# A hybrid SSD and attention block on one core: out_proj's third block of rows is loaded before the attention ends, gate's first operands after it, and a pair of weight casts is queued sooner

## The chip, the cores and the metric

The kernel runs on one core of one Trainium2 chip. The metric is the device time of one execution in microseconds (us); lower is better. The profiler adds its own record of one execution: what each engine did and when. The engines are named as in the profile: PE (TensorE, matrix multiplies), PEld (its weight loads), DVE (VectorE), ACT (ScalarE), POOL (GpSimd) and SP (SyncE, which here only issues DMAs).

## What is computed

One layer of a streaming encoder on a sequence of 1024 tokens of width 1024, all in float32:

```python
h = rms_norm(x, pre_mix_gain)
z, xbc, dt, q, k, v = split(h @ w_in)
y_ssd = ssd_group(z, xbc, dt)          # convolution, chunked state-space scan, gate by silu(z), norm
y_sb  = stick_breaking(q, k, v)        # 8 heads of 64, then a norm over each head
mix = concat([y_ssd, y_sb]) @ w_out    # "out_proj"
x = x + rms_norm(mix, post_mix_gain)
h = rms_norm(x, pre_ffn_gain)
f = (silu(h @ w_gate) * (h @ w_up)) @ w_down
x = x + rms_norm(f, post_ffn_gain)
```

## The kernel before, in words

Every large product keeps float32 accuracy by splitting each operand into a high part (a cast, on ACT, line 74) and a low part (the difference, on DVE, line 75) and adding three matmuls (`mm3`, lines 78 to 80: high by high, high by low, low by high). A matmul here is 128 x 128 by 128 x 512. The kernel is one program without loops at run time; Python writes it out, and a scheduler decides the order of the instructions of each engine by readiness and priority. What an engine does is then strictly in that order. `tc.issue_after(ins)` puts what is written inside it behind `ins` on the engine of `ins`; it is an order, not a wait. `tc.high_priority` moves what is inside it ahead.

The work has these stages, with their times in the profiled execution:

1. *Merged stage*, to about 505 us: in_proj, the SSD group and the attention are interleaved by `merge`, and at its end the first two blocks of out_proj (`stage("wo")` and `stage("o01")`). out_proj works on blocks of 128 tokens, p = 0 to 7, from the end of the sequence. A block needs its eight 128 x 128 pieces of y, normed and split, in a pair of tiles `yhl` (high and low).
2. *out_proj and its norms*, to about 592 us: the loop over p at line 1158. `run(p)` issues block p's 48 matmuls into two PSUM banks `po`; `out_tail(p - 2)` transposes on PE the result of two blocks earlier; `out_norm(p)` loads the block's rows of x, 512 KB, into `x1` (line 1091, SP), squares `po` on ACT (line 1095), makes the norm's factor (lines 913 to 918), multiplies by the gain `gm_b` on DVE (line 1101), adds x (line 1102), squares again (line 1104), stores x1 by POOL (line 1105) and multiplies by `g2_b` (line 1110, tile `tm`, the operand of the transposes). The two gain rows are loaded once, broadcast over 128 partitions to 512 KB each, by DMAs that ACT issues (line 923), and scaled on ACT (line 924).
3. *gate and up*: a Strassen-like scheme of seven products for each pair of feature blocks, a "quad" (`quad`, `step`). Each `step` of a quad takes two operands, gate's and up's, from the list `lops`. The first quad's first operands are `eo` (four loads of 256 KB by `early_load`, cast by `early_ops`); the second's and third's are the `heads` (loaded by `head_load`, cast by `left_gen` when `pump` asks for them).
4. *down*, to the end.

`out_load(p, part)` (lines 801 to 835) brings a block's y in: two loads of y into the low tile of `yhl` (lines 823 and 828, 256 KB each), four loads of norm factors into `Rb` (lines 825 and 832, each row broadcast over 64 or 128 partitions), three multiplies of the two on DVE (lines 826 and 834), the cast on ACT and the difference on DVE. `Rb` has one buffer for all blocks from 1 on (the tile of tag "Rb", line 822), so a block's factors can only be loaded when the difference of the block before it is done.

Where a block's `yhl` lies matters for the change. Block 1, 6 and 7 share two buffers of the pool `wo` (line 813), on the side of the memory where in_proj's weights were, free when in_proj's last matmul is done. Blocks 2 to 5 lie in the tiles of four later operands (line 811: T3h, T3l, T2h, T2l), in a pool that is opened where the attention's tiles were, so they can be written only after the attention's last use of those. The two gain rows, `x1`, `tm` and `eo` lie there too.

`rows_rstd(0, i)` (lines 788 to 799) makes the norm factors `r_d` of the tokens of blocks 4 to 7 from sums that the attention stores last; those of blocks 1 to 3 exist earlier.

Of the kernel before, what the change touches and what calls it, by code (L numbers as in the profile page):

```python
# [48 lines left out]
def tile_hybrid_block(  # L49
# [731 lines left out]
    def load_wo(i):  # L781
        for k, c in enumerate(KO):
            hi, lo = woh[k][i], wol[k][i]
            A.activation(hi, f32(lo), AF.Copy, scale=g_mix[:, c : c + 1])
            V.scalar_tensor_tensor(lo, f32(lo), g_mix[:, c : c + 1], f32(hi), ALU.mult, ALU.subtract)  # L785
            yield 0, 0.6
# [14 lines left out]
    def out_load(p, part):  # L801


        sb = NB - 1 - p
        n, csl = sb // 4, slice(P * (sb % 4), P * (sb % 4) + P)
        if p not in blk:
            if p == 0:
                blk[p] = tuple(big.tile([P, 8, P], F32R, tag=x, name="yhl") for x in ("G", "dec"))
            else:
                if 2 <= p < 6:  # L810
                    yhl = rpA.tile([P, 2, 8, P], F32R, tag=("T3h", "T3l", "T2h", "T2l")[p - 2], name="yhl")
                else:
                    yhl = wo.tile([P, 2, 8, P], F32R, tag="yhl", name="yhl", bufs=2)
                blk[p] = yhl[:, 0], yhl[:, 1]
        yh, yl = blk[p][:2]
        y_v = y_d[n].rearrange("c p s -> p c s")
        g0, g1, k0 = {"early": (0, 1, 0), "late": (1, 2, 6), "all": (0, 2, 0)}[part]
        k1 = 4 + 2 * g1
        if part == "late":
            Rb = pre.tile([P, 2, P], F32, name="Rb2")  # L820
        else:
            Rb = (pre.tile([P, 6, P], F32, name="Rb0") if p == 0 else wo.tile([P, 8, P], F32, tag="Rb", name="Rb"))[:, 0:k1]
            nc.sync.dma_start(f32(yl[:, 0:4]), y_v[:, 4:8, csl])
            for h in range(2):
                nc.sync.dma_start(Rb[64 * h : 64 * h + 64, 0:4], r_d[n][0][4 * h : 4 * h + 4, csl].partition_broadcast(64))
            V.tensor_tensor(Rb[:, 0:4], f32(yl[:, 0:4]), Rb[:, 0:4], ALU.mult)
        kg = 4 + 2 * g0
        nc.sync.dma_start(f32(yl[:, kg:k1]), y_v[:, 2 * g0 : 2 * g1, csl])
        R4 = Rb[:, kg - k0 :].rearrange("p (g k) s -> p g k s", k=2)
        y4 = f32(yl[:, kg:k1]).rearrange("p (g k) s -> p g k s", k=2)  # L830
        for g in range(g0, g1):
            nc.sync.dma_start(R4[:, g - g0, 1], r_d[n][g][8 - 8 * g, csl].partition_broadcast(P))
        for k in range(2):
            V.tensor_tensor(R4[:, :, k], y4[:, :, k], R4[:, :, 1], ALU.mult)
        split(yh[:, k0:k1], yl[:, k0:k1], Rb)
# [12 lines left out]
    def stage(t):  # L848
        nonlocal wo
        if t[0] in "xz" and t < "z2":  # L850

            with tc.issue_after(stored[0].ins):
                next(copied, None)
                if t[0] == "z" or t > "x3":
                    next(copied, None)
        if t[:3] == "qkv":
            yield from proj_qkv(int(t[3]), st[int(t[3])])
        elif t[0] == "x":
            yield from conv_tile(int(t[1]))
        elif t == "ssd":  # L860
            side.append(ssd())
            yield 0, 0.1
        elif t == "z23":
            yield from z_last()
        elif t[0] == "z":
            if t == "z0":
                yield from flush()
            yield from proj(t, z_evac(int(t[1])), 1.8)
        elif t == "r0":
            rows_rstd(1, 0, t2, tag="t2")  # L870
            yield 0, 1
        elif t == "wo":
            yield from flush()
            right_w.close()
            wo = es_w.enter_context(tc.tile_pool(reuse_waits="tile", name="wo", bufs=1, side="right"))
            fetch_wo(1)
            out_load(0, "late")
            out_load(1, "all")
            side.append(load_wo(1))
            yield 0, 3  # L880
        elif t == "o01":
            yield from out_mm(0, (0,), (0, 6))
            yield from out_mm(0, (0,), (6, 8))
            yield from out_mm(1, (0,))
            yield from flush()
            yield from out_mm(0, (1,))
            yield from out_mm(1, (1,))
# [182 lines left out]
    with es_o:  # L1070
# [15 lines left out]
        def out_norm(p):  # L1086
# [1 line left out]
            ssl = slice(P * sb, P * sb + P)  # L1088
            pm = blk.pop(p)[2]
            x1 = op.tile([P, D], F32, tag="x1", name="x1")  # L1090
            nc.sync.dma_start(x1, x[ssl, :])
            ssq = small_p.tile([P, 2], F32, tag="ssq", name="ssq")
            t = op.tile([P, D], F32, tag="tm", name="tm", bufs=2)
            for n in range(2):
# [59 lines left out]
        for i in range(2):  # L1154
            rows_rstd(0, i, op, tag="hT", bufs=1)
        ts = {}
        out_load(2, "all")
        for p in range(NB - 1):
            if p > 1:
                run(p)  # L1160
# [7 lines left out]
            if 2 < p + 2 < NB:  # L1168
                out_load(p + 2, "all")
            if p == 5:  # L1170
                raw = early_load()

        run(NB - 1)
        es_w.close()
# [13 lines left out]
        step(0)  # L1188
        p1_u = evac[0]
        with tc.issue_after(p1_u.ins):  # L1190
            next(tail, None)
        with tc.high_priority(offset=URGENT):
            next(norm)
# [2 lines left out]
        with tc.high_priority(offset=URGENT):  # L1196
            next(norm, None)
        a00 = step(0)
        with tc.issue_after(p1_u.ins):
            pump(2)  # L1200
        step(1)
        p1_u = evac[0]
        with tc.high_priority(offset=URGENT), tc.issue_after(last_mm[0].ins):
# [263 lines left out]
```

## Time and profile before

| | us |
|---|---|
| median of 3 runs | 1236.88 (1235.38 to 1238.39) |
| the profiled execution, its own time | 1237.42 |
| its span, first to last instruction | 1235.7 |
| PE busy | 1193.2 (97% of the span) |
| DVE busy | 929.3 (75%) |
| ACT busy | 588.2 (48%) |
| POOL busy | 92.8 (8%) |
| the 16 DMA engines, over the span | 157 GB/s |

A busy PE is not a PE at its peak: the same matmul is recorded at different lengths and distances, and what counts is how far the starts of neighbouring matmuls lie apart. The views that matter are the list of who waited for whom, cut to a stretch of time; the timeline of one engine; the groups of one tile; and the busy time by window. A row of the timeline has the start in us, the duration, the engine, the line, the operation, what it writes and reads, the count, and in brackets the time the engine stood idle before it and what released it. SPq and ACTq are the DMA issues of SP and ACT.

### The profile page before, as it was taken

To read this page: it belongs to the slowest core of one execution; us is meant where nothing else is said; L and a number is where in the kernel's file an instruction comes from. 1 tells how busy PE (TensorE), PEld (TensorE's weight loads), DVE (VectorE), ACT (ScalarE), POOL (GpSimd) and SP (SyncE) were. 2 spreads that over 40 slices of the span, in tenths; PEclk is the share of its full clock that TensorE was granted. 3 is DMA by queue.
4 is the path that set the end of the run, shared out by engine and by line. 5 is a ranking of instruction groups with operands and counts; after the bars stand their busy time and mean duration, and the time that the engine had idled before them with its cause. 6 is when DMAs were issued, how large, how long until landed. Compare 5 with 4: busy or idle time off the path is not lost.

```text
span 1235.7 us, 16325 instructions
## 1 busy us (share of the span) xinstructions
PE 1193.2 (97%) x5641; PEld 971.1 (79%) x5641; DVE 929.3 (75%) x1466; ACT 588.2 (48%) x1124; POOL 92.8 (8%) x232
## 2 busy tenths in 40 slices
PE   9998999999999999799999999999999999999997
PEld 7776778887887776578788888888888888888885
DVE  7478988778997978366898765565665558998877
ACT  7347555555654677345653333332333325444543
POOL 0041110000100100011200000000000000000000
PEclk9998999999999999899999999999999999999999
DMA  6794464455557345663973223223133298233346
GB/s 192 195 353 125 111 175 132 137 152 177 158 168 199 111 136 148 209 206 134 323 212 128 88 75 103 86 76 94 54 101 102 72 327 308 65 124 105 100 136 238
DMA packets 144731, 189.53 MB, mean 153 GB/s; under 512 B 10900, under 2 KB 97140, under 8 KB 144648
## 3 DMA queue, kind: packets, MB, share of 16 engines
q1 hardware_dynamic: 133392, 157.47, 41.5%
q0 software_dynamic: 7424, 25.17, 5.5%
q10 hardware_dynamic: 3832, 5.84, 1.3%
q8 instruction: 44, 0.72, 0.2%
q14 instruction: 39, 0.32, 0.1%
HBM read 138.52 MB, written 55.16 MB: 157 GB/s over the span
## 4 chain that ended last, share of the span: by engine, by line
PE 74%; DVE 11%; DMA 6%; ACT 4%; issue 3%; SPq 1%; POOL 0%; DVEq 0%; ACTq 0%; POOLq 0%
PE pd L79 5%; PE pd L78 5%; PE pd L80 5%; DVE sn L605 3%; PE o L628 2%; PE tp L616 2%; PE peu L80 2%; PE pcu L80 2%; PE pcg L80 2%; PE peg L80 2%; PE pcg L79 2%; PE peu L78 2%; PE pcu L78 2%; PE peg L79 2%; PE peg L78 2%
## 5 line engine op out<-in xcount | busy, mean ns | idle before, releaser
L74 ACT CAST flhi<-fraw 128x512 fp32r<-128x512 f32 x98 | 60.2, 621 | 153.7 <-PE pcg L79 35.6
L79 PE MATMUL pd<-folo,fohi 128*128 128x512 f32 x260 | 101.4, 390 | 0.2 <-DVE folo L75 0.2
L78 PE MATMUL pd<-fohi 128*128 128x512 f32 x260 | 101.4, 390 | 0.0
L80 PE MATMUL pd<-fohi,folo 128*128 128x512 f32 x260 | 101.2, 389 | 0.0
L605 DVE TENSOR_TENSOR_SCAN sn<-sn,smask 128x1024 f32<-128x1024 f32 (+3 forms) x64 | 87.4, 1366 | 17.8 <-ACT sn L601 17.5
L75 DVE TENSOR_TENSOR fllo<-fraw,flhi 128x512 fp32r<-128x512 f32 x98 | 66.9, 686 | 29.1 <-ACT flhi L74 29.1
L601 ACT ACTIVATE sn<-zp,msc 128x512 f32<-128x512 f32 (+2 forms) x96 | 56.0, 584 | 37.5 <-PE zp L600 33.7
L74 ACT CAST fohi<-rt 128x512 fp32r<-128x512 f32 x83 | 48.7, 618 | 47.7 <-PE pd L79 27.9
L78 PE MATMUL po<-woh,yhl 128*128 128x512 f32 x128 | 52.6, 411 | 10.4 <-ACT yhl L74 10.2
L620 ACT CAST wh<-tp 128x512 fp32r<-128x512 f32 (+1 forms) x80 | 42.6, 544 | 39.0 <-PE tp L616 38.5
L75 DVE TENSOR_TENSOR folo<-rt,fohi 128x512 fp32r<-128x512 f32 x83 | 55.2, 695 | 7.0 <-ACT fohi L74 7.0
L74 ACT CAST flhi<-fs 128x512 fp32r<-128x512 f32 x44 | 27.3, 622 | 69.7 <-PE peg L79 34.9
L621 DVE TENSOR_TENSOR wl<-tp,wh 128x512 fp32r<-128x512 f32 (+1 forms) x80 | 49.8, 628 | 10.5 <-ACT wh L620 10.2
L78 PEld LDWEIGHTS pd<-fohi 128*128 128x128 f32 x260 | 48.8, 188 | 10.6 <-ACT fohi L74 0.4
L79 PEld LDWEIGHTS pd<-folo,fohi 128*128 128x128 f32 x260 | 48.8, 188 | 10.5 <-DVE folo L75 0.5
L602 ACT ACTIVATE sp<-zp,msc 128x512 f32<-128x512 f32 (+2 forms) x96 | 55.8, 582 | 2.5 <-PE tp L616 2.4
L80 PEld LDWEIGHTS pd<-fohi,folo 128*128 128x128 f32 x260 | 48.8, 188 | 10.1
L79 PE MATMUL po<-wol,yhl 128*128 128x512 f32 x128 | 52.1, 407 | 1.2 <-DVE wol L785 1.2
L616 PE MATMUL tp<-ident,sp 128*128 128x128 f32 x288 | 47.9, 277 | 5.4 <-DVE sp L606 4.9
L78 PE MATMUL pj_x<-hh,wh_x 128*128 128x512 f32 x128 | 52.5, 410 | 0.0
L80 PE MATMUL po<-woh,yhl 128*128 128x512 f32 x128 | 51.5, 403 | 0.7 <-DVE yhl L75 0.7
L1065 POOL DMA_DIRECT2D a_d<-sg x44 | 23.8, 540 | 376.9 <-DVE sg L1064 376.8
(426 smaller groups left out, 3474.6 us busy)
## 6 DMA issues: line engine op xcount, KB each, us to landing
ps<-a_d SPq DMA_DIRECT2D x55, 256.0 KB
fraw<-in_w_gate_dram SPq DMA_DIRECT2D x22, 512.0 KB
fraw<-in_w_up_dram SPq DMA_DIRECT2D x22, 512.0 KB
a_d<-sg POOLq DMA_DIRECT2D x44, 256.0 KB, 2.6
rt<-in_w_down_dram SPq DMA_DIRECT2D x33, 256.0 KB
rt<-a_d SPq DMA_DIRECT2D x22, 256.0 KB
ps<-in_w_down_dram SPq DMA_DIRECT2D x22, 256.0 KB
xt<-in_x_t_dram SPq DMA_DIRECT2D x8, 512.0 KB
```

The lines of the kernel that those rows point to most:

```text
L74: A.copy(hi, src)
L75: V.tensor_tensor(lo, src, f32(hi), ALU.subtract)
L78: T.matmul(ps, lhsT=ah, rhs=bh, start=start, stop=False, skip_group_check=more)
L79: T.matmul(ps, lhsT=ah, rhs=bl, start=False, stop=False, skip_group_check=more)
L80: last_mm[0] = T.matmul(ps, lhsT=al, rhs=bh, start=False, stop=stop, skip_group_check=more)
L601: A.activation(sn[:, 1 + off : 1 + off + cw_], zp[:, 0:cw_], AF.Sigmoid, scale=rqn[:, qb : qb + 1])
L602: A.activation(sp[:, off : off + cw_], zp[:, 0:cw_], AF.Sigmoid, scale=rqp[:, qb : qb + 1])
L605: V.tensor_tensor_scan(sn[:, 1 : 1 + W], sn[:, 1 : 1 + W], smask[:, 0:W], 1.0, ALU.mult, ALU.max)
L616: T.transpose(tp[:, P * i : P * i + P], ws[a][:, co : co + P], ident)
L620: A.copy(wh[:, 0:n_], tp[:, 0:n_])
L621: V.tensor_tensor(wl[:, 0:n_], tp[:, 0:n_], f32(wh[:, 0:n_]), ALU.subtract)
L628: T.matmul(o[:, 0:cw_], lhsT=vv[:, k, h, :], rhs=wt[:, c0 : c0 + cw_], start=(first and k == kb + 1 and wt is wh), stop=(last and k == kb ...
```

## The change

Four edits, all around the border of stages 1, 2 and 3:

- Block 2's `yhl` comes from the pool `wo` instead of the tile T3h, so that blocks 1, 2, 6 and 7 share its two buffers; blocks 3, 4 and 5 move up by one tile each (T3h, T3l, T2h), and T2l is no longer used for this.
- `out_load(2, "all")` is called in the merged stage, right after block 1's, instead of after the attention.
- `early_load`, the four loads of `eo`, is put on SP behind the load of x of block 5 (`stored[0]` now remembers the last load of line 1091).
- The casts of the second quad's heads, made by `pump(2)` after the second `step(0)`, are made by `pump(3)` after the first, so that they stand one step earlier in the program.

One line is added in `stage`, so the lines from there to the end of `out_norm` and `out_tail` have numbers one higher in the changed kernel (1101 becomes 1102).

```diff
--- before.py
+++ after.py
@@ -807,8 +807,8 @@
             if p == 0:
                 blk[p] = tuple(big.tile([P, 8, P], F32R, tag=x, name="yhl") for x in ("G", "dec"))
             else:
-                if 2 <= p < 6:
-                    yhl = rpA.tile([P, 2, 8, P], F32R, tag=("T3h", "T3l", "T2h", "T2l")[p - 2], name="yhl")
+                if 3 <= p < 6:
+                    yhl = rpA.tile([P, 2, 8, P], F32R, tag=("T3h", "T3l", "T2h")[p - 3], name="yhl")
                 else:
                     yhl = wo.tile([P, 2, 8, P], F32R, tag="yhl", name="yhl", bufs=2)
                 blk[p] = yhl[:, 0], yhl[:, 1]
@@ -877,6 +877,7 @@
             out_load(0, "late")
             out_load(1, "all")
             side.append(load_wo(1))
+            out_load(2, "all")
             yield 0, 3
         elif t == "o01":
             yield from out_mm(0, (0,), (0, 6))
@@ -1088,7 +1089,7 @@
             ssl = slice(P * sb, P * sb + P)
             pm = blk.pop(p)[2]
             x1 = op.tile([P, D], F32, tag="x1", name="x1")
-            nc.sync.dma_start(x1, x[ssl, :])
+            stored[0] = nc.sync.dma_start(x1, x[ssl, :])
             ssq = small_p.tile([P, 2], F32, tag="ssq", name="ssq")
             t = op.tile([P, D], F32, tag="tm", name="tm", bufs=2)
             for n in range(2):
@@ -1154,7 +1155,6 @@
         for i in range(2):
             rows_rstd(0, i, op, tag="hT", bufs=1)
         ts = {}
-        out_load(2, "all")
         for p in range(NB - 1):
             if p > 1:
                 run(p)
@@ -1168,7 +1168,8 @@
             if 2 < p + 2 < NB:
                 out_load(p + 2, "all")
             if p == 5:
-                raw = early_load()
+                with tc.issue_after(stored[0].ins):
+                    raw = early_load()
 
         run(NB - 1)
         es_w.close()
@@ -1188,6 +1189,7 @@
         step(0)
         p1_u = evac[0]
         with tc.issue_after(p1_u.ins):
+            pump(3)
             next(tail, None)
         with tc.high_priority(offset=URGENT):
             next(norm)
@@ -1196,8 +1198,6 @@
         with tc.high_priority(offset=URGENT):
             next(norm, None)
         a00 = step(0)
-        with tc.issue_after(p1_u.ins):
-            pump(2)
         step(1)
         p1_u = evac[0]
         with tc.high_priority(offset=URGENT), tc.issue_after(last_mm[0].ins):
```

The scheduler turns this into other orders on the engines. Three places follow; in each, what stands there before and what stands there now. The numbers at the ends of names tell tiles of one name apart.

SP, from the attention's last store of y (line 635) on. `yhl_5245` is block 2's, `yhl_5330` with `Rb_5331` block 3's, `x1_5258` and `x1_5294` are the rows of x of blocks 0 and 1, `rt0` is the tile in which `rows_rstd` makes its factors. Before:

```order
L635 DMA y_d0_108<-osb3_4073 128x512
L823 DMA yhl_5684<-y_d0_108 128x4x128
L1078 DMA eo_5816<-eo_d0_146 128x512
L1078 DMA eo_5818<-eo_d1_147 128x512
L1078 DMA eo_5820<-eo_d2_148 128x512
L792 DMA rt0_5227<-ss_d09_130 36x128
L823 DMA yhl_5245<-y_d1_109 128x4x128
L828 DMA yhl_5245<-y_d1_109 128x4x128
L1091 DMA x1_5258<-in_x_dram 128x1024
L1091 DMA x1_5294<-in_x_dram 128x1024
L823 DMA yhl_5330<-y_d1_109 128x4x128
L799 DMA r_d09_134<-rt0_5227 36x128
```

Now:

```order
L635 DMA y_d0_108<-osb3_4073 128x512
L792 DMA rt0_5240<-ss_d09_130 36x128
L1092 DMA x1_5258<-in_x_dram 128x1024
L1092 DMA x1_5294<-in_x_dram 128x1024
L823 DMA yhl_5330<-y_d1_109 128x4x128
L825 DMA Rb_5331<-r_d19_136 64x4x128 x2
L799 DMA r_d09_134<-rt0_5240 36x128
L828 DMA yhl_5330<-y_d1_109 128x4x128
L832 DMA Rb_5331<-r_d19_136 128x128
L832 DMA Rb_5331<-r_d11_137 128x128
L792 DMA rt1_5249<-ss_d01_131 4x128
L823 DMA yhl_5448<-y_d0_108 128x4x128
```

The three eo loads and block 2's two loads of y have left this place, and block 3's loads of factors (`Rb_5331`), which stood behind the second `rt` load, now stand ahead of it.

DVE, the last rows ahead of block 3's difference (line 75, the last row). `x_5258` and `x_5294` are blocks 0 and 1, `tm<-po` is line 1101 or 1102 of block 1, `Rb<-yhl,Rb` are block 3's multiplies. Before:

```order
L915 SCALAR_TENSOR_TENSOR v<-ssq,e 128x1
L798 TENSOR_TENSOR rt_5236<-rt_5236 4x128
L916 SCALAR_TENSOR_TENSOR t<-y_5283,v 128x1
L916 SCALAR_TENSOR_TENSOR t<-y_5301,v 128x1
L918 SCALAR_TENSOR_TENSOR r<-t,y_5283 128x1
L834 TENSOR_TENSOR Rb<-yhl,Rb 128x2x128
L1110 SCALAR_TENSOR_TENSOR tm<-x_5258,r,g_b 128x512 x2
L918 SCALAR_TENSOR_TENSOR r<-t,y_5301 128x1
L834 TENSOR_TENSOR Rb<-yhl,Rb 128x2x128
L1101 SCALAR_TENSOR_TENSOR tm<-po,r,gm_b 128x512 x2
L1102 TENSOR_TENSOR x_5294<-x_5294,tm 128x512 x2
L75 TENSOR_TENSOR yhl<-Rb,yhl 128x1024
```

Now:

```order
L834 TENSOR_TENSOR Rb<-yhl,Rb 128x2x128
L798 TENSOR_TENSOR rt_5249<-rt_5249 4x128
L916 SCALAR_TENSOR_TENSOR v<-ssq_5274,e 128x1
L916 SCALAR_TENSOR_TENSOR v<-ssq,e 128x1
L917 SCALAR_TENSOR_TENSOR t<-y_5283,v 128x1
L917 SCALAR_TENSOR_TENSOR t<-y_5301,v 128x1
L919 SCALAR_TENSOR_TENSOR r<-t,y_5283 128x1
L919 SCALAR_TENSOR_TENSOR r<-t,y_5301 128x1
L1111 SCALAR_TENSOR_TENSOR tm<-x_5258,r,g_b 128x512 x2
L1102 SCALAR_TENSOR_TENSOR tm<-po,r,gm_b 128x512 x2
L1103 TENSOR_TENSOR x_5294<-x_5294,tm 128x512 x2
L75 TENSOR_TENSOR yhl<-Rb,yhl 128x1024
```

Block 3's second multiply (the first row; the first multiply stands two rows above it) stands now ahead of the factors of both blocks, and no longer behind block 0's line 1110, so that the cast on ACT that reads both can run earlier. The difference stands, as before, behind block 0's line 1110 (now 1111) and block 1's four operations.

ACT, around the casts of the second quad's heads (`flhi<-head`). `tm_6021` is block 7, `hT` are copies of transposes. Before:

```order
L1104 ACTIVATE tm_6021,ssq2_6100<-x1_6018 128x512 x2
L913 ACTIVATE e_6140<-ssq2_6100 128x1
L74 CAST T2h_5214<-pt_6025 128x4x128
L914 ACTIVATE y0_6138<-ssq2_6100,e_6140 128x1
L74 CAST T3h_5216<-pt_6031 128x4x128
L1125 COPY hT_6108<-pt_6110 128x512
L1125 COPY hT_6109<-pt_6116 128x512
L74 CAST flhi_6173<-head_6010 128x512
L74 CAST flhi_6177<-head_6012 128x512
L74 CAST flhi_6181<-head_6014 128x512
L74 CAST flhi_6185<-head_6016 128x512
L1063 ACT_TABLE_LOAD
```

Now:

```order
L1105 ACTIVATE tm_6021,ssq2_6116<-x1_6018 128x512 x2
L914 ACTIVATE e_6156<-ssq2_6116 128x1
L74 CAST flhi_6080<-head_6010 128x512
L915 ACTIVATE y0_6154<-ssq2_6116,e_6156 128x1
L74 CAST flhi_6084<-head_6012 128x512
L74 CAST flhi_6088<-head_6014 128x512
L74 CAST flhi_6092<-head_6016 128x512
L74 CAST T2h_5227<-pt_6025 128x4x128
L74 CAST T3h_5229<-pt_6031 128x4x128
L1126 COPY hT_6124<-pt_6126 128x512
L1126 COPY hT_6125<-pt_6132 128x512
L1064 ACT_TABLE_LOAD
```

The four head casts stand ahead of the two T2 and T3 casts and of the two copies `hT` that they stood behind.

## The prediction

> **What bounds the kernel now.** The first lines of the profile's page say that PE is nearly always occupied, so a gain can only come from the few places where it stands still or runs at a lower clock.
>
> ```profile
> span 1235.7 us, 16325 instructions
> PE 1193.2 (97%) x5641; PEld 971.1 (79%) x5641; DVE 929.3 (75%) x1466; ACT 588.2 (48%) x1124; POOL 92.8 (8%) x232
> ```
>
> Next the waits of PE alone, cut to the stretch that the change touches: the first two rows from 500 to 600 us (out_proj), the last two from 590 to 690 (gate). Columns: total, times, longest.
>
> ```profile
> PE po L78 <- ACT yhl L74: 10.2, 2, 8.1
> PE po L80 <- DVE yhl L75: 0.7, 2, 0.5
> PE pag L80 <- DVE fllo L75: 1.2, 1, 1.2
> PE pag L78 <- ACT flhi L74: 0.3, 1, 0.3
> ```
>
> So PE waits 10.9 us for blocks of out_proj (yhl) and 1.5 us for head casts. PE's timeline says where:
>
> ```profile
> 504.92 0.39 PE L80 MATMUL po<-woh,yhl 128*128 128x512 f32 x1
> 513.39 0.80 PE L78 MATMUL po<-woh,yhl 128*128 128x512 f32 x1 [8.09 <-ACT yhl L74]
> 519.10 0.47 PE L80 MATMUL po<-woh,yhl 128*128 128x512 f32 x1
> 529.42 0.50 PE L80 MATMUL po<-woh,yhl 128*128 128x512 f32 x1 [0.54 <-DVE yhl L75]
> 539.77 1.03 PE L1124 MATMUL pt<-ident,tm 128*128 128x128 f32 x8
> 542.97 0.67 PE L78 MATMUL po<-woh,yhl 128*128 128x512 f32 x1 [2.16 <-ACT yhl L74]
> 544.23 0.80 PE L80 MATMUL po<-woh,yhl 128*128 128x512 f32 x1 [0.16 <-DVE yhl L75]
> 556.66 0.48 PE L78 MATMUL po<-woh,yhl 128*128 128x512 f32 x1
> ```
>
> Block 2 starts 8.09 us late. The one at 519.10 is the thirteenth after its first, so these are 0.44 us apart; the 45 left of block 3's 48, from 529.42 to 539.77, are 0.23 us apart. So after a long wait PE runs at about half pace for 5.7 us, which costs 13 x 0.21 = 2.7 us more. Block 3 starts in earnest at 529.42 and block 4 at 544.23; block 5 comes with no wait. A block undisturbed takes 48 x 0.23 = 11.0 us, with its transposes 12.0.
>
> **Part by part: block 2 earlier.** Its inputs were late because the tile lay in the attention's memory. Its factors were on their way long before:
>
> ```profile
> 490.99 1.24 SPq L825 DMA_DIRECT2D Rb<-r_d  x2
> 498.70 1.40 SPq L1078 DMA_DIRECT2D eo<-eo_d  x3
> 515.75 1.24 SPq L825 DMA_DIRECT2D Rb<-r_d  x2
> 529.39 1.55 SPq L825 DMA_DIRECT2D Rb<-r_d  x2
> 531.00 1.95 SPq L832 DMA_DIRECT2D Rb<-r_d  x2
> 507.73 0.22 DVE L793 TENSOR_SCALAR rt<-rt 36x128 f32<-36x128 f32 x1 [14.16 <-DMA rt<-ss_d]
> 536.01 0.69 DVE L826 TENSOR_TENSOR Rb<-yhl,Rb 128x512 f32<-128x512 f32 x1 [3.09 <-DMA Rb<-r_d]
> 538.17 0.43 DVE L834 TENSOR_TENSOR Rb<-yhl,Rb 128x256 f32<-128x256 f32 x1 [1.15 <-DMA Rb<-r_d]
> 542.95 1.23 DVE L75 TENSOR_TENSOR yhl<-Rb,yhl 128x1024 fp32r<-128x1024 f32 x1 [0.78 <-ACT yhl L74]
> ```
>
> Block 4's factors, issued from 529.39 to 532.95, were used at 538.17: 5.2 us after the last issue. The same for block 2, whose four issues end at about 493.5 (490.99 and twice 1.24), gives 498.7. Then two multiplies (0.43 each), the cast (at most the difference's 1.23) and the difference (1.23): ready at about 502, PE asks at 505.3 (504.92 + 0.39). DVE stood idle for the 14.16 us before 507.73, so the work is free there; without that cover DVE's part would cost 2.8 us (0.69 + 0.86 + 1.23). The two added loads of y stand on SP ahead of block 0's and 1's last factors, about 0.47 us of issue each (1.40 / 3 in eo's row); I take 0 for them, at most 1. The 8.09 us and the 2.7 of low pace go, and block 2 ends at 505.3 + 11.0 = 516.3.
>
> **What is late next: block 3.** Before, it was ready 529.42 − 516.3 = 13.1 us later than that. Its difference stands on DVE behind block 0's whole norm and block 1's first half (the order shows this, before and now). That chain begins with the gain rows:
>
> ```profile
> 499.63 0.39 ACTq L923 DMA_DIRECT2D gm_b<-in_post_mix_gain_dram  x1
> 501.14 0.36 ACTq L923 DMA_DIRECT2D g_b<-in_pre_ffn_gain_dram  x1
> 510.71 1.06 ACT L924 ACTIVATE g_b<-g_b 128x1024 f32<-128x1024 f32 x1 [1.41 <-DMA g_b<-in_pre_ffn_gain_dram]
> 513.25 0.59 ACT L1095 ACTIVATE tm<-po 128x512 f32<-128x512 f32 x1
> 515.84 1.41 DVE L1101 SCALAR_TENSOR_TENSOR tm<-po,r,gm_b 128x512 f32<-128x512 f32 x2
> 518.73 0.22 DVE L793 TENSOR_SCALAR rt<-rt 4x128 f32<-4x128 f32 x1 [1.48 <-DMA rt<-ss_d]
> 523.56 0.42 DVE L834 TENSOR_TENSOR Rb<-yhl,Rb 128x256 f32<-128x256 f32 x1 [1.57 <-issue]
> 528.15 1.22 DVE L75 TENSOR_TENSOR yhl<-Rb,yhl 128x1024 fp32r<-128x1024 f32 x1
> 1018.61 0.34 ACTq L923 DMA_DIRECT2D gp_b<-in_post_ffn_gain_dram  x1
> 1025.31 1.06 ACT L924 ACTIVATE gp_b<-gp_b 128x1024 f32<-128x1024 f32 x1 [3.02 <-DMA gp_b<-in_post_ffn_gain_dram]
> ```
>
> Before, g_b landed 9.6 us after its issue (510.71 − 501.14) while the eo loads were under way; gp_b, later and almost alone, took 6.7 (1025.31 − 1018.61). Now block 2's cast stands on ACT ahead of both issues, so they go out at about 500.5 and 501. Without the 768 KB of eo, I take 8.5 us for the second, between those two: landed at 509.5 (507.7 to 510.6). Scaling it takes 1.06 us, so block 0's squares begin at 510.6. From the squares to r and line 1101 took 2.6 us (515.84 − 513.25): 513.2. From line 1101 to the difference's start took 12.3 (528.15 − 515.84). Of these 3.05 were the waits of 1.48 and 1.57 that the rows show; block 3's factors left SP from 515.75 on, now they and the second `rt` load stand right behind the loads of x, some six us earlier, so I take both waits as gone. Line 826 of block 3 (0.69 in its row above) stood in this stretch and stands now ahead of block 0's norm. 12.3 − 3.05 − 0.7 = 8.55, and from the difference's start to PE's row 1.27 (529.42 − 528.15): 513.2 + 8.55 + 1.27 = **523.0**, from 521.2 (g_b at 507.7) to 526.1 (both waits stay).
>
> The transposes ahead of block 3 need block 0's `tm`, which comes four operations of block 1 and the difference ahead of that, at about 519. So PE stands for most of 516.3 to 523.0: some 5.5 us in two or three pieces take the place of 8.09 + 0.54. Against 529.42 that is **6.4 us** earlier.
>
> **Block 4.** Its factors wait for the one buffer, that is for block 3's difference. Before, it started 544.23 − 529.42 = 14.8 us after block 3. PE alone needs 12.0, 13.4 if the pace is as low as after 542.97. Now DVE does both multiplies ahead of block 2's norm and the cast goes ahead of the squares: from 538.17 the way to the end of the difference was 6.0 us (542.95 + 1.23 − 538.17) with some 2.7 of norm in between (line 1101's 1.41, and line 1102's two), and about 4.7 remain, 1.3 less. Against this SP now issues block 2's x and block 7's two loads of y, 1 MB, just ahead of these factors: 0 to 3 us, I take 1. So 14.5 after 523.0 is 537.5, **6.7 us** earlier than 544.23. From block 5 on, before had no wait, and the interval of 12.4 to 556.66 stays. This part lies between 2 us (block 3 at 526.1, block 4 two more late) and 12 (block 3 without a wait at 517.3).
>
> **eo later.** The four loads now stand behind block 5's x, and ahead of block 7's factors.
>
> ```profile
> 559.32 0.41 SPq L1091 DMA_DIRECT2D x<-in_x_dram  x1
> 583.39 2.17 ACT L74 CAST eo<-eo 128x512 fp32r<-128x512 f32 x4
> ```
>
> Block 5's x went out 24 us ahead of eo's casts, and both move with the blocks: time enough for 1 MB, since g_b's 0.5 MB took 9.6 us at the worst. I cost the move at nothing, and the four issues ahead of block 7's factors at 0 to 1 us: they wait for block 6's difference anyway.
>
> **Heads.** Rows around gate's second quad:
>
> ```profile
> 604.44 2.20 ACT L74 CAST flhi<-head 128x512 fp32r<-128x512 f32 x4
> 606.88 0.68 DVE L75 TENSOR_TENSOR fllo<-head,flhi 128x512 fp32r<-128x512 f32 x1
> 605.13 0.50 PE L78 MATMUL pag<-B11h,flhi 128*128 128x512 f32 x1 [0.30 <-ACT flhi L74]
> 607.62 0.50 PE L80 MATMUL pag<-B11h,fllo 128*128 128x512 f32 x1 [1.24 <-DVE fllo L75]
> 613.91 1.03 PE L1124 MATMUL pt<-ident,tm 128*128 128x128 f32 x8
> ```
>
> PE was free at 605.13 − 0.30 = 604.83; 24 matmuls at 0.23 would end at 610.3, and they end at 613.91: 3.6 us of waits and low pace. Now the casts stand four operations earlier on ACT, each about 0.55 us (2.20 / 4): at 602.2. The first difference stands on DVE ahead of five operations of block 7 and its tail that it stood behind, 3.4 us at 0.68 and more with line 1110's two: at about 602.9, done at 603.6. PE finds both at 604.83. Line 1110 of block 7 comes behind three differences, at about 606.5 done, and its transposes are due at 610.3. The T2 and T3 casts that slip back by 2 us are needed only when quad 0 resumes, 72 matmuls later. I take **3.6 us**, from 1 (the wait moves to the next operand) to 3.6.
>
> **The sum.** 6.7 + 3.6 = 10.3 us. The profiled execution took 1237.42, 0.54 over the median, so one like it would take 1227.1, and the median comes from 1236.88 to **1226.6**.
>
> **Rivals.** *Block 3 doesn't wait* (chance 0.17): if block 0's norm is through sooner than I think, block 3 starts at 517.3 and block 4 14.8 later, both 12.1 earlier; with the heads 15.7, or 1221.2. For it speaks that 8.5 us of the new chain are DMA time that I could not read off; against it that even gp_b, almost alone, took 6.7.
>
> *The gain rows land no sooner* (0.19). ACT's loads may not have been held up by SP's eo loads, since SP has a megabyte of x out in any case. Then g_b takes 9.6 us from 501, and block 3 and 4 start 1.1 us later; if one of the two waits stays too, 2.6 later. The gain is 9.2 to 7.7, about 1228.4. [...]
>
> *The heads' wait only moves* (0.10): the next operand, such as the copy of a first product that the second one in its bank must wait for, is late by 2.5 us: 6.7 + 1.1, or 1229.1.
>
> *Block 2 is still late* (0.05): the memory is not free or its factors take ten us longer, and PE waits as before. Then the heads alone are left, 1233.3, or 1235.8 where their wait moves too (0.03 of it).
>
> *Slower* (0.04): block 2's cast stands on ACT ahead of the issue of both gain rows. If its factors are late, PE waits for block 2, and all norms, transposes and block 3 wait for the gain rows besides. It turns to a measurable loss when that cast ends later than 500.5 + 10.3 + 2.5 = 513.3; at 515 the time would be 1241. Against it stand the 5.2 us above.
>
> **How the numbers follow.** The forecast has 0.45. A measurement of this kernel tells 0.2% (2.5 us) from no change, hardly less. Faster: 0.45 + 0.17 + 0.19 + 0.10 + 0.02 = 0.93; same 0.03; slower 0.04. The range reaches from 1221.0 (block 3 without a wait) to 1231.5 (3 us from the blocks and 2.4 from the heads) and leaves out less than 0.2.
>
> **What would show it.** In the profile after: block 2 starts within 1 us of the merged stage's end and runs at 0.23 us a matmul; PE waits 4 to 7 us in front of block 3, for block 0's `tm` and then for DVE's difference; block 4 starts 13.5 to 16 us after block 3; there is no wait of PE on head casts. I am wrong if block 2 waits over 2 us, if block 3 starts in earnest outside 521.2 to 526.1, or if a wait of over 2 us appears after 560.

## The result, and the profile after

The changed kernel took 1229.95 us, the median of five runs (1227.64 to 1232.07), beside 1238.00 of before in five runs (1235.38 to 1238.39): a ratio of 0.9938, 95% interval 0.9918 to 0.9958. Run again among the experiments below, against other runs of before (median 1236.37), it gave 0.9935 (0.9923 to 0.9948). So it is faster by 8.0 us; the forecast was 10.3. The profiled execution took 1227.73 with a span of 1226.0, that is 9.7 less than the span of before.

The page's head and PE's waits from 500 to 690 us, the stretch from which the waits of before were cut (total, times, longest):

```profile
span 1226.0 us, 16335 instructions
...
PE 1188.4 (97%) x5641; PEld 969.5 (79%) x5641; DVE 929.7 (76%) x1466; ACT 588.5 (48%) x1124; POOL 92.8 (8%) x232
```

```profile
PE pt L1125 <- DVE tm L1111: 2.6, 1, 2.6
PE po L80 <- DVE yhl L75: 2.6, 2, 1.8
PE po L78 <- ACT yhl L74: 1.2, 1, 1.2
```

Of 12.4 us of waits 6.4 are left, and none of them is on a head cast or later than block 4. PE's timeline of after has the rows that answer to those of before:

```profile
495.46 1.02 PE L497 MATMUL nps<-nsq,sel 128*2 128x512 f32 x2
...
519.74 1.97 PE L1125 MATMUL pt<-ident,tm 128*128 128x128 f32 x8 [2.62 <-DVE tm L1111]
...
524.06 0.51 PE L80 MATMUL po<-woh,yhl 128*128 128x512 f32 x1 [0.71 <-DVE yhl L75]
...
536.46 0.50 PE L78 MATMUL po<-woh,yhl 128*128 128x512 f32 x1 [1.22 <-ACT yhl L74]
...
539.04 0.50 PE L80 MATMUL po<-woh,yhl 128*128 128x512 f32 x1 [1.84 <-DVE yhl L75]
...
541.66 0.63 PE L79 MATMUL po<-wol,yhl 128*128 128x512 f32 x1
...
605.09 1.03 PE L1125 MATMUL pt<-ident,tm 128*128 128x128 f32 x8
```

Block 2 has no row with a wait: its matmuls follow one another at 0.23 us and end at 517.1. Then PE waits ahead of block 0's transposes (2.62) and for block 3's difference (0.71), and twice for block 4 (1.22 and 1.84). The row at 541.66 stands in a stretch with seven steps of 0.43 us, and the last row is the transposes behind gate's second quad (before: 613.91). The first row is the last norm sum of the merged stage; it serves as the zero below.

In what is ahead of blocks 3 and 4 on ACT, DVE and SP one reads why:

```profile
501.34 1.05 ACT L74 CAST yhl<-Rb 128x1024 fp32r<-128x1024 f32 x1 [4.24 <-DVE Rb L834]
...
501.81 0.44 ACTq L924 DMA_DIRECT2D g_b<-in_pre_ffn_gain_dram  x1
...
510.04 1.06 ACT L925 ACTIVATE g_b<-g_b 128x1024 f32<-128x1024 f32 x1 [1.62 <-DMA g_b<-in_pre_ffn_gain_dram]
511.01 0.58 ACT L1096 ACTIVATE tm<-po 128x512 f32<-128x512 f32 x1
...
502.43 1.23 DVE L75 TENSOR_TENSOR yhl<-Rb,yhl 128x1024 fp32r<-128x1024 f32 x1 [1.12 <-ACT yhl L74]
...
512.84 0.69 DVE L826 TENSOR_TENSOR Rb<-yhl,Rb 128x512 f32<-128x512 f32 x1 [7.50 <-DMA Rb<-r_d]
...
514.15 1.41 DVE L1102 SCALAR_TENSOR_TENSOR tm<-po,r,gm_b 128x512 f32<-128x512 f32 x2
...
522.79 1.22 DVE L75 TENSOR_TENSOR yhl<-Rb,yhl 128x1024 fp32r<-128x1024 f32 x1
...
534.45 0.42 DVE L834 TENSOR_TENSOR Rb<-yhl,Rb 128x256 f32<-128x256 f32 x1 [1.22 <-DMA Rb<-r_d]
...
503.68 1.35 SPq L825 DMA_DIRECT2D Rb<-r_d  x2
...
522.25 0.36 SPq L1092 DMA_DIRECT2D x<-in_x_dram  x1
...
523.13 0.51 SPq L828 DMA_DIRECT2D yhl<-y_d  x1
524.03 1.97 SPq L825 DMA_DIRECT2D Rb<-r_d  x2
526.06 2.83 SPq L832 DMA_DIRECT2D Rb<-r_d  x2
```

Block 2's cast (501.34) and difference (502.43) are early. The scaling of g_b starts 8.2 us after its issue (510.04 − 501.81). On DVE something else is late by almost as much: line 826 of block 3 waited 7.50 us for factors whose issues ended at 505.03, and it stands ahead of block 0's norm, so that line 1102 came at 514.15. Block 4's factors left SP only from 524.03 to 528.89, behind block 2's x (522.25) and block 7's y (523.13), and were used at 534.45.

**A zero that takes out the start.** The times at which the fourteen profiled executions of this study (after was profiled twice) reach the same first norm sum (line 497, some 425 us into the span, with all work before it alike) go from 424.26 to 428.00. The medians of before in four sets of runs lie between 1236.37 and 1238.00, and single runs of one kernel as far as 8.7 us apart. A good part of the spread is thus made before the change begins, and blocks are better compared from the last norm sum on than by their place in the span:

| us after the last norm sum | before | after | after, second time | earlier (first) | forecast |
|---|---|---|---|---|---|
| block 3 in earnest | 34.97 | 28.60 | 28.40 | 6.37 | 6.4 |
| block 4 in earnest | 49.78 | 43.58 | 43.19 | 6.20 | 6.7 |
| block 5 | 62.21 | 56.54 | 56.16 | 5.67 | 6.7 |
| gate's first product | 98.34 | 92.29 | 91.48 | 6.05 | 6.7 |
| transposes behind gate's second quad | 119.46 | 109.63 | 108.79 | 9.83 | 10.3 |
| end of the span | 741.25 | 730.54 | 730.33 | 10.71 | 10.3 |

(Block 3 after, for instance: 524.06 − 495.46.) The two executions of after agree within 0.9 us at every row.

### The profile page after: what moved, and what is told of

Same layout as the page of the kernel before. It is cut to its first block, busy times and chain, and to the rows that moved or that the text cites. A ratio compares the mean times of both kernels' runs of the same rounds, so it can differ in the third digit from the quotient of the medians.

```text
span 1226.0 us, 16335 instructions
## 1 busy us (share of the span) xinstructions
PE 1188.4 (97%) x5641; PEld 969.5 (79%) x5641; DVE 929.7 (76%) x1466; ACT 588.5 (48%) x1124; POOL 92.8 (8%) x232
## 4 chain that ended last, share of the span: by engine, by line
PE 76%; DVE 11%; DMA 4%; ACT 4%; issue 3%; SPq 1%; POOL 0%; DVEq 0%; ACTq 0%; POOLq 0%
PE pd L80 5%; PE pd L78 5%; PE pd L79 5%; DVE sn L605 3%; PE tp L616 2%; PE o L628 2%; PE pag L78 2%; PE pag L79 2%; PE pcg L79 2%; PE peg L79 2%; PE pau L78 2%; PE peu L78 2%; PE peu L79 2%; PE pau L79 2%; PE pcu L78 2%
```

## The experiments

Theory: block 2's 8.1 us of wait and its low pace go, and the gain ends where block 3 meets block 0's norm, which waits for gain rows and for block 3's factors. Rivals: that eo's move, or something else ahead of block 3, does it. The first four kernels do one part alone, or all but one.

**Block 2 alone** (the new `out_load(2, "all")` in the merged stage and its tile; nothing else).

> Only block 2 is moved; eo and the head casts stay as before. Theory (block 3 waits for block 0's norm, which begins with the gain rows, and the eo loads slow those rows): block 2 without a wait, g_b in use some 9.6 us after its issue instead of 8.2, block 3 in earnest at about 525.5, block 4 also later than in the full change because eo's loads stand among its factors; 2.5 to 3.5 us faster than before. Rival (what eo does beside them changes nothing): block 3 at 524.1 and block 4 at 539.0 as in the full change, 4.3 us faster.

Measured: 0.9962 (0.9948 to 0.9976), 4.7 us. Block 3's row is 30.0 after the norm sum, block 4's 41.7 without a wait. g_b was used 8.0 us after its issue, with eo's loads under way as in before, where it was 9.6. So the size is the rival's, and the part of the theory by which the eo loads slow the gain rows got no support. Block 3 itself stands 1.4 us later than in the full change (30.0 against 28.6), near the theory's place. What was later there were its factors: line 826 came 19.8 us after the norm sum (515.03 − 495.22) instead of 17.4 (512.84 − 495.46).

**Heads alone.**

```diff
         with tc.issue_after(p1_u.ins):
+            pump(3)
             next(tail, None)
...
         a00 = step(0)
-        with tc.issue_after(p1_u.ins):
-            pump(2)
         step(1)
```

> Only the head casts are moved. Theory: the two waits on flhi and fllo and the low pace behind them go, 3.5 to 3.9 us faster than before and nothing else moves. Rival (the heads gain only because gate begins earlier in the full change, or the wait moves to the next operand): 1 us or less, with a wait of PE on another operand of the second quad.

Measured: 0.9984 (0.9973 to 0.9995), 2.0 us, and no wait of PE at the second quad. Direction right, size below the forecast. The two kernels in which the heads stay (block 2 alone, and the next) tell why. Their rows of the second quad, block 2 alone first, then before:

```profile
602.00 0.50 PE L80 MATMUL pag<-B11h,fllo 128*128 128x512 f32 x1 [1.23 <-DVE fllo L75]
602.34 0.39 PE L78 MATMUL pag<-B11h,flhi 128*128 128x512 f32 x1
```

```profile
608.34 0.63 PE L79 MATMUL pag<-B11l,flhi 128*128 128x512 f32 x1
608.77 0.63 PE L80 MATMUL pag<-B11h,fllo 128*128 128x512 f32 x1
```

The waits are the same to 0.02 us (0.29 and 1.23, and 0.28 and 1.23; in before 0.30 and 1.24). But in before eight matmuls behind them, from 608.34 to 611.33, come 0.43 apart, and here 0.23. In before the granted clock says the same: 1.00 from 606 to 608 us, 0.58 from 608 to 612. From the first B21h product on eo to that on the head it takes 15.57 us in before, 13.94 and 13.93 in these two, 11.78 where the casts come sooner. So the waits are worth 2.2 us, and the other 1.6 were a low pace that came behind the same waits in one execution and not in two others. What brings it on is not shown: it came behind two waits of together 1.54 us in before, and didn't come behind 1.52 and 1.51 in the two others.

**eo alone** (line 1172's `issue_after` and `stored[0]`).

> Only the eo loads are moved. Theory: g_b is in use 8.2 to 8.5 us after its issue instead of 9.6, but block 3 waits for PE's late block 2, so 0 to 0.5 us faster than before. Rival (the eo move is the part that earns): 1.5 us or more faster. Other rival (it costs, since the loads now stand ahead of block 7's factors): slower by 0.5 to 1 with a wait at block 7.

Measured: 0.9979 (0.9969 to 0.9990), 2.6 us: the rival was right, and the theory wrong. g_b was ready without a wait of its own, its scaling 5.6 us after the issue (508.34 − 502.73), and PE waited 4.16 us for block 2 instead of 8.09. Where block 2 is still loaded late, eo's loads stand ahead of its y on SP (its factors left SP before them); without them its first matmul comes 15.0 us after the norm sum (512.09 − 497.08), with them 16.3 in the kernel with the heads alone (514.11 − 497.82) and 18.9 in before. These two have the same order of work up to there, so single traces put eo's part only between 1.3 and 3.9 us; the 2.6 are the medians'.

**All but eo.**

> The change with the eo loads back at their old place. Theory: g_b and block 3's factors land 1 to 2 us later than in the full change, block 3 in earnest at 525 to 526, 1.5 to 2.5 us slower than the full change, about 1232. Rival (gain rows land no sooner without eo): block 3 at 524 and the same time as the full change within 0.5.

Measured: 0.9943 (0.9928 to 0.9959), the same as the full change. Its rows for the gain row, block 3's factors and difference, block 1's norm, and block 4:

```profile
502.00 0.45 ACTq L924 DMA_DIRECT2D g_b<-in_pre_ffn_gain_dram  x1
...
509.32 1.06 ACT L925 ACTIVATE g_b<-g_b 128x1024 f32<-128x1024 f32 x1 [0.76 <-DMA g_b<-in_pre_ffn_gain_dram]
...
514.15 0.69 DVE L826 TENSOR_TENSOR Rb<-yhl,Rb 128x512 f32<-128x512 f32 x1 [2.34 <-DMA Rb<-r_d]
...
519.93 1.23 DVE L75 TENSOR_TENSOR yhl<-Rb,yhl 128x1024 fp32r<-128x1024 f32 x1 [0.33 <-ACT yhl L74]
...
536.32 0.48 PE L78 MATMUL po<-woh,yhl 128*128 128x512 f32 x1
```

With eo back the gain row came sooner (7.3 us after its issue, 8.2 in the full change), the factors 1.7 later, counted from the norm sum (19.1 us behind it instead of 17.4). Block 3 begins 29.3 us after it, behind PE waits of 3.23 and 1.58, instead of 28.6. The difference of block 3 now stands ahead of block 1's norm (519.93, and line 1102 at 522.85; in after 522.79 behind 520.27), and block 4 begins at 536.32 with no wait; waits of 1.37 and 0.59 further on give back part of this. So eo's move is worth 2.6 us alone and nothing that the medians show once block 2 is early. There it is a trade: block 3 comes 0.7 us sooner, but block 4 waits 3.1 us (1.22 and 1.84) that it doesn't wait with eo in its old place, where SP issues most of block 4's factors from 521.19, ahead of block 2's x at 523.52. That is read from one execution of each.

The next four act on what is ahead of block 3. The windows of after show the stretch: the last two columns are the mean busy share of the DMA engines and GB/s.

```profile
core 0: us, PE busy (x) PEld busy (x) DVE busy (x) ACT busy (x) POOL busy (x), PEclk, DMA share, GB/s
...
500.00:504.00 4.00, 4.00 (x19) 3.32 (x18) 2.20 (x4) 2.52 (x3) 0.00 (x0) 1.00 0.50 149
504.00:508.00 4.00, 4.00 (x19) 3.30 (x19) 1.07 (x4) 0.76 (x2) 0.00 (x0) 1.00 0.96 325
508.00:512.00 4.00, 4.00 (x20) 3.30 (x19) 0.00 (x0) 2.38 (x5) 0.00 (x0) 1.00 1.15 280
```

From 504 to 512 us the DMA engines are full: two x, two gain rows, the factors and y of block 3; at 325 and 280 GB/s some 2.4 MB pass.

**Early gm_b.**

```diff
...
+            early_gain.append(hp.tile([P, D], F32, tag="R_b", name="gm_w"))
+            with tc.issue_after(rb_last[0].ins): nc.sync.dma_start(early_gain[0], post_mix_gain[0].partition_broadcast(P))
             out_load(2, "all")
...
+            with tc.issue_after(cast_1.ins): A.mul(early_gain[0], early_gain[0], -0.5)
...
```

> The change, and the first gain row (gm_b, 512 KB) is loaded and scaled already in the merged stage, into memory that the projections left; block 7 alone uses a second copy loaded at block 5. Theory (block 3 waits for block 0's norm, whose start is set by 1 MB of gain rows and by block 3's factors, all in the stretch from 503 to 512 us where the DMA engines are full): g_b in use at about 507 instead of 510, block 3's factors at about 511.3 instead of 512.8, block 3 in earnest at 518.5 to 520 instead of 524.1, block 4 without a wait, 4 to 7 us faster than the full change, 1223 to 1226. Rival (something else holds block 3, for instance the DVE work of the norms): block 3 at 523 or later and within 1.5 us of the full change.

Measured: 0.9902 (0.9884 to 0.9920), median 1224.66, clear of the full change's second interval (0.9923 to 0.9948), though not of its first (0.9918 to 0.9958). The sizes are near those of the theory:

```profile
501.29 0.37 ACTq L928 DMA_DIRECT2D g_b<-in_pre_ffn_gain_dram  x1
...
506.63 1.06 ACT L929 ACTIVATE g_b<-g_b 128x1024 f32<-128x1024 f32 x1 [1.56 <-DMA g_b<-in_pre_ffn_gain_dram]
...
509.02 1.41 DVE L1105 SCALAR_TENSOR_TENSOR tm<-po,r,gm_w 128x512 f32<-128x512 f32 x2
...
511.54 0.68 DVE L826 TENSOR_TENSOR Rb<-yhl,Rb 128x512 f32<-128x512 f32 x1
...
520.04 0.50 PE L80 MATMUL po<-woh,yhl 128*128 128x512 f32 x1 [1.69 <-DVE yhl L75]
```

g_b alone is used 5.3 us after its issue, line 1105 (1102 there) at 509.02 instead of 514.15, block 3's line 826 waits for nothing, and block 3 is at 520.04, 24.7 after the norm sum instead of 28.6. It still waits 1.69 us for its difference and block 4 waits 0.52, where the theory had no wait; two waits for `tm` further on (1.27 and 1.57) give some back.

**Early gm_b, and g_b off the first root.** The scaling is queued behind `rsq[0]` of block 0 instead of at its load.

> As the one with the early gm_b, and besides the scaling of the second row, g_b, stands on ACT behind block 0's first root instead of ahead of it. Theory (it is the landing of the rows that starts the norm, and of the two the first that used them): block 0's line 1102 no longer waits for g_b and comes 2 to 4 us earlier still, at 506 to 508; block 3 at 518 or PE's own end of block 2, 0 to 2 us faster than the one with gm_b alone. Rival (block 3's factors, not the norm, are what is last by then): the same time within 1 us.

Measured: 0.9899 (0.9882 to 0.9917), the same. Block 0's line came 11.4 us after the norm sum, 2.3 sooner (505.74 − 494.35), yet block 3 24.3 after it instead of 24.7, with DVE waiting 1.24 and 1.66 for block 3's factors. The rival: by then the factors are last.

**Block 3's loads first.**

```diff
-                out_load(p + 2, "all")
+                with tc.high_priority(offset=URGENT) if p == 1 else nullcontext():
+                    out_load(p + 2, "all")
```

> The change, with block 3's loads, multiplies, cast and difference ahead of block 0's and 1's x and of block 0's norm; the gain rows stay late. Theory (what PE waits for ahead of block 3 is the order of the work and full DMA engines, not block 3's own work): block 3's difference is done before PE asks (by 514), but x goes out some 4 us later, so that the wait moves to block 0's tm (519 to 521); 1 to 4 us faster than the full change. Rival (block 3's own factors are the limit, and nothing else): block 3 begins at 517.5 without a wait and the kernel is 6 us or more faster.

Measured: 0.9955 (0.9938 to 0.9972), where 1 to 4 us faster than the full change was expected. It isn't faster; by the ratios it is 2.5 us slower, but the two intervals overlap. That the wait moves to block 0's tm was right (4.88 us in front of the transposes), the size was not. SP stood at block 3's factors, which wait for the one buffer, with x behind them, and x went out 11.1 us after the norm sum instead of 5.7. But it wasn't x that held block 0's norm: the add of x on DVE (522.30) waits for nothing. Its line 1102 came only at 521.44, 21.2 us after the norm sum instead of 18.7, behind block 0's root on ACT; and that stood in ACT's order behind block 3's cast, which waited for block 3's factors:

```profile
517.94 1.05 ACT L74 CAST yhl<-Rb 128x1024 fp32r<-128x1024 f32 x1 [4.83 <-DVE Rb L834]
...
520.52 0.28 ACT L915 ACTIVATE y<-ssq,e 128x1 f32<-128x1 f32 x1
...
521.44 0.74 DVE L1102 SCALAR_TENSOR_TENSOR tm<-po,r,gm_b 128x512 f32<-128x512 f32 x1
```

Block 3 is 28.2 after the norm sum, as late as before the edit.

**Block 1's x behind block 3's factors.**

> The change, with block 1's x (512 KB) behind block 3's factors on SP. Theory (queues take turns, so SP's own order sets the factors and not the gain rows): block 3's factors in use at 511 to 511.5 instead of 512.8, g_b unchanged at about 510. Rival (all transfers share the full engines by amount): g_b 1.5 us sooner too, at 508.5. By either, block 3's difference now stands ahead of block 1's norm on DVE, so block 3 at 520 to 522 instead of 524.1 and 1 to 3 us faster than the full change, unless block 1's tm is then late for block 4.

Measured: 0.9901 (0.9879 to 0.9923), by the ratios 4 us faster than the full change, with intervals that just touch. Factors in use 15.2 us after the norm sum instead of 17.4, g_b 7.2 us after its issue instead of 8.2. That did not bring block 0's norm sooner: line 1102 stands 19.4 us after the norm sum (518.78 − 499.38) instead of 18.7, since DVE waited 2.22 us more for the second part of the factors. What came sooner is block 3's difference, 22.1 us after the norm sum instead of 27.3 and now ahead of block 1's norm, because the edit also writes the loads and the difference of block 3 ahead of it; block 3 begins 26.8 us after the norm sum instead of 28.6. On the queues: with 512 KB less on SP ahead of block 3's factors, both came sooner, the factors by 2.2 us and g_b by 1.0, which is the rival's direction. With 512 KB more on SP (all but eo) only the factors came later, by 1.7 us; g_b came 0.9 sooner (7.3 us after its issue instead of 8.2). In the full change it took 8.2 both times. The runs do not settle how the two queues share the engines: the theory's reading and the rival's were both assumptions.

**Block 2's x and the y of blocks 5 to 7 behind block 4's factors.**

> The change, with block 2's x and the y of blocks 5 to 7 behind block 4's factors on SP; gain rows, block 3 and the order on ACT stay. Theory (the transfers ahead of block 4's factors on SP cost block 4 its wait): block 3 as before at 524, block 4's factors in use 1.5 to 2.5 us sooner after block 3's difference than in the full change (13.1 us from the end of line 826 of block 3's pair to that of block 4 there), PE's 3.1 us of waits for block 4 fall under 1.5; 1 to 2.5 us faster than the full change. Rival (those loads cost nothing, block 4 waits for DVE): block 4 15 us behind block 3 as now, the same time within 0.5.

Measured: 0.9918 (0.9903 to 0.9932), by the ratios 2.1 us faster than the full change, with intervals that overlap a little.

```profile
523.64 0.50 PE L80 MATMUL po<-woh,yhl 128*128 128x512 f32 x1 [0.73 <-DVE yhl L75]
...
534.55 0.48 PE L78 MATMUL po<-woh,yhl 128*128 128x512 f32 x1
...
524.92 1.10 SPq L832 DMA_DIRECT2D Rb<-r_d  x2
526.12 1.03 SPq L1092 DMA_DIRECT2D x<-in_x_dram  x2
```

Block 3 begins as in after, block 4 10.9 us behind it instead of 15.0 and without a wait, 4.1 us less. Of these 2.9 are the factors: line 826 comes 6.7 us after the start of block 3's difference (529.06 − 522.36) instead of 9.6 (532.41 − 522.79). The other 1.2 are the place of block 4's difference on DVE, which the edit also puts ahead of block 2's adds of x. Two waits for `tm` further on (1.33 and 0.33) give some back.

**A second buffer for block 3's factors.**

```diff
-  ... else wo.tile([P, 8, P], F32, tag="Rb", name="Rb"))[:, 0:k1]
+  ... else hp.tile([P, 8, P], F32, tag="R_b", name="Rb3") if p == 3 else wo.tile([P, 8, P], F32, tag="Rb", name="Rb"))[:, 0:k1]
```

> The change, with block 3's factors in a second buffer, so that their loads go out right behind block 2's, ahead of the x; the gain rows stay as late as they are. Theory (gain rows and block 3's factors are late by nearly the same; of the two the gain rows stay): line 1102 of block 0 still at 512.5 to 513.6, but block 3's difference now ahead of block 1's norm, block 3 at 521 to 522.5, 1.5 to 3 us faster than the full change. Rival (block 3's factors alone held DVE and all behind it): line 1102 at 511 or earlier, block 3 at 519.5 or earlier, 4 us or more faster.

Measured: 0.9908 (0.9892 to 0.9923), 3.3 us faster than the full change.

```profile
510.44 0.69 DVE L826 TENSOR_TENSOR Rb<-yhl,Rb 128x512 f32<-128x512 f32 x1 [5.25 <-DMA yhl<-y_d]
...
513.70 1.41 DVE L1102 SCALAR_TENSOR_TENSOR tm<-po,r,gm_b 128x512 f32<-128x512 f32 x2
...
516.36 1.21 DVE L75 TENSOR_TENSOR yhl<-Rb,yhl 128x1024 fp32r<-128x1024 f32 x1
...
520.57 0.48 PE L78 MATMUL po<-woh,yhl 128*128 128x512 f32 x1
```

The factors no longer hold DVE (line 826 waits for y, at 510.44), and line 1102 still comes at 513.70, since g_b is late. What is gained is the place of the difference, 516.36, ahead of block 1's norm: block 3 at 520.57, 25.5 after the norm sum. This is the theory, near its numbers; the rival's 511 did not come.

**All of it** (the early gm_b, x of blocks 1 and 2, y of blocks 4 to 7 behind the next block's factors).

> The early gm_b together with the x of blocks 1 and 2 and all y of blocks 4 to 7 behind the factors of the block that is next. Theory (amount of transfers from 503 to 512 us and their order on SP are all that is left ahead of blocks 3 and 4): block 3 in earnest at 518 to 519.5, block 4 without a wait or under 0.6, 0 to 3 us faster than the early gm_b alone, 1221.5 to 1224.5. Rival (x that late makes block 1's and 2's norms late instead): a wait on tm of over 2 us ahead of block 3 or 4, and no gain over the early gm_b.

Measured: 0.9910 (0.9895 to 0.9926): no gain over the early gm_b. Block 3 is 23.0 after the norm sum, the best of all, but blocks 4 and 5 wait 0.89 and 0.40 for `tm` and 2.20 for a difference. The rival, in a milder form.

**The full change once more.**

> The full change once more, beside the others on one chip. Expected: the same ratio as the first time within the intervals, 0.992 to 0.996, and if its profiled execution is later at the last norm sum of the merged stage than 495.9, later at every block by the same.

Measured: 0.9935 (0.9923 to 0.9948). The last norm sum is 1.5 us later in the span (496.97), blocks 3 to 5 are 1.1 to 1.3 later and gate 0.7: by nearly the same.

## Why the prediction was right, and where it was off

Right in kind and within its range, 1229.95 against 1226.6 (1221.0 to 1231.5). Point by point:

- **Block 2.** Its cast and difference came at 501.34 and 502.43 (forecast: ready about 502), with no wait and no low pace, and the block was through at 517.1 (forecast 516.3), the norm sum being 1.0 later than in before. The y loads on SP, taken at 0: the merged stage from first to last norm sum is 70.5 us after and 69.8 before, within the 68.8 to 72.4 of all kernels, so no cost can be seen.
- **Block 3.** 6.4 us forecast, 6.37 measured from the norm sum. Two errors inside cancelled: g_b took 8.2 us (8.5 assumed), but squares to line 1102 took 3.1 instead of 2.6, since the multiply with block 3's factors, which I let stand there without a wait, waited 7.50. The wait of PE ahead of the block, 4 to 7 us by the prediction, was 3.3 (2.62 and 0.71): the rest of the stretch held the transposes and matmuls at the low pace (matmuls 0.43 to 0.57 us apart). The reason given for 8.5, that eo's absence speeds the row, got no support beside an early block 2: the row took 8.0 and 7.3 with eo's loads there, 8.2 both times without. Beside a late block 2 it may hold: 9.6 and 7.5 with them, at most 5.6 without. So the rival "the gain rows land no sooner" fits the early block 2, but its price does not, and the cause stays open. The prediction's comparison with gp_b as a row that loads almost alone doesn't carry: in that window of before, 1016 to 1026 us, the DMA engines were full (1.05 of their time, 396 GB/s), and a row that really was alone on ACT's queue took 4.7 to 5.6 in later runs.
- **Block 4.** The mis-sized term: "0 to 3 us, I take 1" for the x and y ahead of its factors. From the start of block 3's difference to the last multiply with block 4's factors (line 834) it is 11.7 us after (534.45 − 522.79) and was 10.0 in before (538.17 − 528.15), so the term measured 1.6. The piece behind that, to block 4 in earnest, took 4.5 instead of 6.0. The interval was thus 15.0, not 14.5. Moving x and y out of the way later earned 2.9 of the 11.7. And the low pace behind it took another 0.5: 12.96 from block 4 to block 5, not the 12.4 that I carried over. Hence 5.7 at block 5 and 6.0 at gate instead of 6.7.
- **eo.** Nothing that the medians show in the full change, as forecast; but 2.6 us alone, which the forecast did not see.
- **Heads.** No wait is left, as forecast. In the pair of profiled executions it is worth 3.8 us (15.57 to 11.78), by the medians 2.0 (0.6 to 3.3): 1.6 of it was a low pace that came in one of three executions with the same waits. This, with a stall near the end of before's profiled execution, far behind the change,

```profile
1213.34 0.49 PE L78 MATMUL pd<-fohi 128*128 128x512 f32 x1
1214.06 0.50 PE L79 MATMUL pd<-folo,fohi 128*128 128x512 f32 x1 [0.23 <-DVE folo L75]
```

may account for the difference between the 10.7 us of the two traces and the 8.0 of the medians: from the transposes behind gate's second quad to the end after gained 0.9 (10.71 − 9.83), and 10.7 − 1.6 − 0.9 = 8.2. That is an account and not shown. The same stall stands in six of the fourteen profiled executions, one of the full change's two among them, so the 0.9 is at least in part scatter; and how often before's executions have the low pace is not on record. A simpler sum needs neither: the 6.0 of gate, and 2.0 for the heads by the medians, make the 8.0.

So two terms of the sum were off. One is block 4's, 1.6 us instead of 1, with 0.5 of low pace behind it. The other is the price of the heads, 3.6 instead of 2.0: it was read from one execution, together with a low pace that two others with the same waits don't have. The rivals: block 3 did wait (2.62 and 0.71 us), the heads' wait did not move on, block 2 was not late, and the time was not longer.

## What to carry to other kernels

When several loads meet in a stretch where the DMA engines are full (here 0.96 and 1.15 of their time), look there for what can go out before it or after it: moving 512 KB out of it, or x behind the factors that the next block needs, earned 2 to 4 us by the ratios, up to half of the change itself. Such a move can also change the order on DVE, as it did twice here, and part of the gain is then that. Price a wait of a microsecond or so apart from the low pace behind it, since the pace may come in some executions only (here in one of three). And compare traces from a landmark just ahead of the change, not from the span's start.

## What the runs showed of the hardware that was not expected

- The same two waits (0.3 and 1.2 us) were followed by eight matmuls 0.43 us apart in one execution (granted clock 0.58) and by none in two others (0.23 us apart). Elsewhere in the traces from 500 to 620 us, single waits of 1.3 to 1.7 us ahead of a product were followed by none, and the six of 1.84 to 2.20 us each by five to seven such steps.
- The first 256 KB of a block's factors were in use 7.8 us after the end of their issue in block 3 (512.84 − 505.03), where the DMA engines were full (0.96 and 1.15 of their time), and 4.2 in block 4 of the run in which x and y stood behind them (529.06 − 524.87).
- A row of 512 KB was in use 4.7 to 5.6 us after its issue when it was alone on ACT's queue (three runs), mostly 7.2 to 8.5 behind another row, though 5.1 in the run in which x left SP late, 5.6 with eo alone moved, and 9.6 in before. How the two queues share the engines stays open. Whether both gain rows early would do better was not tried.
- Several ways out of the same stretch (early gm_b, late x, second buffer) each earned 3 to 4 us over the full change by the ratios, and two of them together no more than one: the next wait stands close behind. The best kernels of the study are the two with the early gm_b and the one with block 1's x late (0.9899 to 0.9902), which the intervals can't tell apart: 4 us faster than the full change and 12 faster than before.
